# Heads 1 to 3: one weight sum by VectorE instead of an adding transfer, first splits of v two steps sooner, other spacing of the moves

## The chip, the cores and the metric

The kernel runs on one core of one Trainium2 chip. The metric is the device time of one execution in microseconds (us), the median of several runs. The core has a matrix engine (TensorE, PE in the profile), VectorE (DVE), ScalarE (ACT), GpSimd (POOL) and SyncE (SP); SP, ACT and POOL also issue transfers (DMAs), each through a queue of its own, onto the same 16 DMA engines.

## The reference

One decoder block over 512 tokens with a model width of 1024: a gated short convolution and an mLSTM branch with 4 heads read the same normalised input, are merged by sigmoid gates, and a gated embedding follows. Cut to what matters here:

```python
hn = rmsnorm(x, g_mix)
proj = einsum('bsd,de->bse', hn, w_in)
(xa, ba, ca, za, q, k, v, o, zb, ig, fg, ga, gb) = split(proj, ...)
ya = ba * causal_short_conv(ca * xa, conv_w, conv_b)
ya = einsum('bsc,cd->bsd', ya * silu(za), w_a_out)
hb = rmsnorm(mlstm_chunkwise(q, k, v, ig + b_i, fg + b_f), g_head)
yb = einsum('bsv,vd->bsd', sigmoid(o) * hb * silu(zb), w_b_out)
merged = sigmoid(ga) * ya + sigmoid(gb) * yb
x = x + einsum('bsd,de->bse', merged, w_o)
x = x + sigmoid(einsum(rmsnorm(x, g_ple), w_ple_gate)) * einsum(p, w_ple)
out = rmsnorm(x, g_final)
```

All of it is float32. Each head has 256 columns of q and k and 512 columns of v and o.

## The kernel before, in words

**Three matmuls for one.** A float32 operand is split into a high part, which TensorE takes exactly, and a low part, the rest. ScalarE writes the high part (`whi`, line 180) and VectorE subtracts it from the source (`wlo`, line 181); `mm3` (lines 231 to 235) multiplies high by high, high by low and low by high (L233, L234, L235 in the profile).

**Seven products for eight.** Most weight blocks come in pairs, and `pair` with `strassen` multiplies a 2 x 2 arrangement of blocks with seven products (a Strassen-Winograd scheme). The four weight chunks b11, b21, b12, b22 of a pair are 512 x 512 (1 MB each). For v and o of head h, b11 and b21 are the two halves in depth of v's weights, b12 and b22 those of o's. The seven right-hand operands are, in this order: operand 0, b11; operand 1, b21; operand 2, b11+b12; operand 3, b22; operand 4, that plus b22; operand 5, b12+b22; operand 6, operand 4 plus b21. So there are four sums, each made in place in a chunk's buffer (`wraw`, four buffers). A sum that `pair` marks None is an adding transfer: GpSimd issues a DMA (`add_chunk`, line 156) that reads the chunk from HBM once more and adds it to what lies in the buffer, in two halves of 512 KB. A sum that it marks `dve` is a VectorE addition of two buffers, in two halves too (line 185).

**The order of the work** is written out by hand. Product j has two halves, i = 0 and 1, for the two upper blocks of 128 tokens; after the matmuls of a half comes one *step* (`step` and `tick`), so that a pair has 14 steps, s1 to s14. In a step come, in this order: the tasks newly handed over (copies out of PSUM), one half of the split of the next operand (`split_half`: the high part on ACT, the low part on DVE, then the sums that hang on that operand), and one advance of every generator in `active`, the oldest first. Operand j+1 is therefore split in the two steps of product j, and the adds of an operand follow directly on its split. The sums hang on the operands so: b11+=b12 on operand 0; b12+=b22 on operand 1 where it is a transfer and on operand 3 where it is VectorE's; b11+=b22 on operand 2; b11+=b21 on operand 4. The loads of the next chunks are issued by SP (line 148) as soon as an operand's last use is past (`done`). Every engine runs its instructions in the order in which they were written.

**The stages.** `head(h)` runs four times. In heads 0 and 2 the pair v/o is followed by a pair for the gate zb of this and the next head and then by a pair for the merge gates (`sink_gate`); between heads 1 and 2 lies a pair for q and k. While the v/o pair runs, `scores` (started with it) makes the decay-weighted scores on ACT, DVE and, with 96 matmuls of up to 512 columns over the heads, PE; `scored` (line 990) then has GpSimd load the stored gate of an odd head (`gty` from `z_d`, line 994).

**sink_vo** (line 971) takes the results of the v/o pair. For v (n == 0) it waits for some steps (4 for the first two token blocks of heads 1 to 3), takes the buffer `vv`, splits the result into it (line 978 on ACT, line 981 on DVE) and leaves it for the weighted sums. For o it multiplies sigmoid(o) into the gate (lines 983 to 987). The copy of token block 0 is handed over in s3, its sum `c` is made in s4, its sink starts in s5; with 4 waiting steps the split stands in s9, that of block 1 in s10.

**finish(h)** (line 840) turns the finished head into the layout that the last projection wants: VectorE transposes 32 x 32 blocks (`turn`, line 812) into a buffer `yc`, 16 *moves* copy blocks within it (line 821 on ACT, line 819 on DVE; for head 3 into the buffer `m`), and `put` (line 824) stores the result in HBM (`yt_d`). `yc` and `vv` share one buffer (tag "vv"): the next head's `vv` can only be written when the stores of `yc` have read it. For heads 0 and 2 `finish` does half the tokens in 8 steps of moves, stores them (`put(0)`), transposes the other half and moves it in 6 steps that ACT and DVE share; its last store is issued by ACT in s3 of the next head's v/o pair. Head 1's two stores are issued by ACT in s3 of head 2's v/o pair. Head 3's moves run in the first pair of the convolution stage, from s9 on; that stage's `ya` (lines 408 and 410) shares the two tags "qk" and "vv". `recut` (heads 1 and 3) reads q and k back from HBM and splits them.

The list of moves is a list of pairs, one a step: (moves on ACT, moves on DVE).

Of the kernel before, what the change touches and what calls it, by code (L numbers as in the profile page):

```python
# [22 lines left out]
DV = 512  # L23
# [4 lines left out]
Q, K, V, O, ZB = 4096, 5120, 6144, 8192, 10240  # L28
# [8 lines left out]
def hybrid_block(ctx, tc, x, p, g_mix, w_in, conv_w, conv_b, w_a_out, b_gates, g_head,  # L37
# [24 lines left out]
    w_in_v = w_in[0].rearrange("(kt p) n -> p kt n", p=P)  # L62
# [9 lines left out]
    def chunk(view, k0, pieces):  # L72
        got, pos = [], 0
        for c, n in pieces:
            got.append((view[:, k0:k0 + HC, c:c + n], slice(0, HC), slice(pos, pos + n)))
            pos += n
        chunks.append(got)
        return len(chunks) - 1
# [5 lines left out]
    def pair(view, p1, p2, on_dve=0):  # L84

        where = ((p1, 0), (p1, HC), (p2, HC), (p2, 0)) if on_dve == 2 else ((p1, 0), (p1, HC), (p2, 0), (p2, HC))
        b11, b21, b12, b22 = (chunk(view, k, p) for p, k in where)
        if on_dve == 2:  # L90
            b12, b22 = b22, b12
        e2, e3 = (dve if on_dve >= n else None for n in (2, 1))
        t3 = [(b12, b22, e3)]
        operands.extend([(b11, [(b11, b12, None)]), (b21, [] if e3 else t3), (b11, [(b11, b22, e2)]),
                         (b22, t3 if e3 else []), (b11, [(b11, b21, e2)]), (b12, []), (b11, [])])
# [6 lines left out]
    qk_block(1)  # L102
    qk_block(0)
    for h in range(NH):
        pair(w_in_v, [(V + h * DV, DV)], [(O + h * DV, DV)])
        if h % 2 == 0:
            pair(w_in_v, [(ZB + h * DV, DV)], [(ZB + (h + 1) * DV, DV)])
            pair(w_in_v, [((GB, GA)[h // 2], CW)], [((GB, GA)[h // 2] + CW, CW)], 2)
        elif h == 1:
            pair(w_in_v, *([(Q + i * DK, DK), (K + i * DK, DK)] for i in (2, 3)), 1)  # L110
# [126 lines left out]
    def cut(hi, lo, src, scale=None):  # L237

        if scale is None:
            act.activation(hi, src, AF.Copy)  # L240
            dve.tensor_tensor(lo, src, hi.bitcast(F32), ALU.subtract)
        else:
            act.activation(hi, src, AF.Copy, scale=scale)
            dve.scalar_tensor_tensor(lo, src, scale, hi.bitcast(F32), ALU.mult, ALU.subtract)
# [38 lines left out]
    def temp(tag, name=None, dt=F32):  # L283

        return tp.tile([P, S], dt, name=name or tag, tag=tag, bufs={"c": 3}.get(tag, 2))
# [509 lines left out]
    def ptile(u, j, t):  # L795
        a = POFF[j] + (t - j) * P
        return u[:, a:a + P]
# [30 lines left out]
    def moves(move, plan):  # L828

        todo = deque(range((P // B) ** 2))  # L830
        for n_act, n_dve in plan:
            for i in range(max(n_act, n_dve)):
                if i < n_act:
                    move(todo.popleft(), False)
                if i < n_dve:
                    move(todo.popleft(), True)
            yield
        assert not todo

    def finish(h, y, tools):  # L840

        turn, move, put, _ = tools or turning(h, False, m[:, :2, :] if h == NH - 1 else None)
        if h % 2 == 0:
            yield from moves(move, [(2, 0), (2, 0), (3, 0), (3, 0), (2, 0), (1, 0), (2, 0), (1, 0)])
            put(0)
            for t in (2, 3):
                turn(y, t)
                yield
            yield from moves(move, [(1, 2), (1, 2), (0, 2), (0, 2), (1, 2), (1, 2)])
            put(1, nc.scalar)  # L850
            return
        for _ in range(4):
            yield
        for ts in ((0,), (1,), (2,), (3,)) if h == 1 else ((0, 1), (), (2,), (3,)):
            for t in ts:
                turn(y, t)
            yield
        yield from moves(move, [(1, 1)] * 8 if h == 1 else [(3, 0), (3, 1), (2, 1), (1, 1), (2, 2)])
        for i in range(2):
            put(i, nc.scalar if h == 1 else nc.gpsimd)  # L860

    def qk_tile():
        both = hp.tile([P, 2, 4, S], F32R, name="qk", tag="qk", align_bytes=256)
        return [both[:, i] for i in range(2)]
# [83 lines left out]
    def head(h, qk):  # L948
        vv = []

        def sink_qk(n, t, src):

            fs, ps = slice(2 * (t % 2), 2 * (t % 2) + 2), slice(t // 2 * H2, (t // 2 + 1) * H2)
            src = src.rearrange("p (f s) -> p f s", f=2)
            if n == 1:
                nc.gpsimd.dma_start(qk_d[h + 1][:, fs, ps], src)
                return
            for _ in range(4 if t < 2 else 0):
                yield
            if not qk:  # L960
                qk.extend(qk_tile())
            cut(*[u[:, fs, ps] for u in qk], src)
            yield

        if h == 2:
            strassen(hn_lhs, sink_qk, True)
        pr = [hq2.tile([P, 1280], F32R, name=f"pr{i}", align_bytes=256) for i in range(2)]
        pp = hq2.tile([P, 1280], F32, name="pp")
        gt = []

        def sink_vo(n, t, src):
            if n == 0:
                for _ in range(4 if t < 2 and h else 0):
                    yield
                if not vv:
                    both = hp.tile([P, 2, NT, DV], F32R, name="vv", tag="vv", align_bytes=256)
                    vv.extend(both[:, i] for i in range(2))
                act.activation(vv[0][:, t, :], src, AF.Copy)
                if t < 2:
                    yield  # L980
                dve.tensor_tensor(vv[1][:, t, :], src, vv[0][:, t, :].bitcast(F32), ALU.subtract)
            elif h % 2:
                so = temp("e", "so")
                act.activation(so, src, AF.Sigmoid)
                dve.tensor_tensor(gt[0][:, t, :], gt[0][:, t, :], so, ALU.mult)
            else:
                act.activation(gt[0][:, t, :], src, AF.Sigmoid)
            yield

        def scored():  # L990
            both = hp.tile([P, 2, NT, DV], F32, name="gty", tag="qk", align_bytes=256)
            gt.extend(both[:, i] for i in range(2))
            if h % 2:
                nc.gpsimd.dma_start(gt[0], z_d[h])

        active.append(scores(h, qk, pr, pp, scored))
        strassen(hn_lhs, sink_vo)
        gt, y = gt

        def weighted_sum(t, ps):  # L1000
            dve.tensor_scalar(y[:, t, :], ps, inv[:, t:t + 1], None, ALU.mult)
            junk = temp("e", "junk")
            act.activation(junk, y[:, t, :], AF.Square, accum_out=hss[:, t:t + 1])
            yield

        for t in range(NT):
            ps = ps_x.tile([P, S], F32, name="pv", tag="x")
            for j in range(t + 1):
                mm3(ps, [ptile(u, j, t) for u in pr], [u[:, j, :] for u in vv], j == 0, j == t)
            step(weighted_sum(t, ps))  # L1010

        def norm(t):
            dve.scalar_tensor_tensor(y[:, t, :], y[:, t, :], hr[:, t:t + 1], gt[:, t, :], ALU.mult, ALU.mult)

        def rsqrt():
            a, r, e = htmp
            dve.tensor_scalar(a, hss, 1.0 / DV, EPS, ALU.mult, ALU.add)
            pool.tensor_tensor(r, a, mhalf, ALU.pow)
            yield
            newton(e, a, r)  # L1020
            dve.tensor_tensor(hr, r, e, ALU.mult)
            for t in range(NT) if h % 2 else ():
                norm(t)
                if t == 1:
                    yield

        def sink_z(n, t, src):
            sz = temp("e", "sz")
            act.activation(sz, src, AF.Sigmoid)
            if n == 1:  # L1030
                dve.tensor_tensor(src, sz, src, ALU.mult)
                nc.gpsimd.dma_start(z_d[h + 1][:, t, :], src)
                yield
                return
            dve.tensor_tensor(sz, sz, src, ALU.mult)
            dve.tensor_tensor(gt[:, t, :], gt[:, t, :], sz, ALU.mult)
            yield
            norm(t)
            yield
            if t < 2:  # L1040
                yield
                if not tools:
                    tools.extend(turning(h, True))
                tools[0](y, t)
                yield

        tools = []
        active.append(rsqrt())
        if h % 2 == 0:
            strassen(hn_lhs, sink_z)  # L1050
        return y, tools
# [462 lines left out]
```

## Time and profile before

| | |
|---|---|
| median of 3 runs | 847.54 us (846.37 to 850.4) |
| profiled execution, whole | 846.08 us |
| its span, first to last instruction | 844.0 us |
| PE busy | 829.3 us (98%) |
| DVE busy | 673.2 us (80%) |
| ACT busy | 526.0 us (62%) |
| POOL busy | 219.6 us (26%) |
| DMA traffic | 173.87 MB |

Times in the profile are us from the first instruction. A row of the timeline is: start, duration, engine, line, operation, output <- inputs with their shapes, and in brackets the idle time of the engine before it with what ended it. A group's row is: line, engine, operation, shapes, count | busy us, mean ns of one | idle time before. A matmul's shown duration (0.39 us for 512 columns) overlaps that of the next: while nothing is waited for, such matmuls start every 0.23 us, so a delay of up to some 0.16 us between two of them doesn't show as idle time.

### The profile page before, as it was taken

Reading aid. Unit: us, or ns where it says so; the run is one execution under the profiler, and the core shown is the slowest. Engines: PE = TensorE matmul, PEld = TensorE weight load, DVE = VectorE, ACT = ScalarE, POOL = GpSimd, SP = SyncE. Lnnn points to the kernel's source line nnn. Section 1 sums busy time; section 2 is a strip of 40 time slices with the busy share of each in tenths; the row PEclk is TensorE's granted clock in tenths of the full one; section 3 lists DMA queues with packets and bytes.
Section 4 is the critical chain, followed back from the end, with each engine's and each line's share of the span. In section 5 each row is a group of like instructions: output and inputs, shape, how many; then the busy total and the mean of one; then the engine's idle time right before and its main releaser. Section 6 shows DMA issues by size and latency. Waiting matters only on the chain.

```text
span 844.0 us, 12126 instructions
## 1 busy us (share of the span) xinstructions
PE 829.3 (98%) x4520; PEld 720.5 (85%) x4520; DVE 673.2 (80%) x931; ACT 526.0 (62%) x779; POOL 219.6 (26%) x219
## 2 busy tenths in 40 slices
PE   9999999999999999999999999999999999999996
PEld 7888888888889978888877999999998888888885
DVE  5788767998688758789859899897985687999565
ACT  6467665778655766567766585555457356667553
POOL 5203122214125321320412234433411212121031
PEclk9999999999999999999999999999999999999999
DMA  9748789769979898995997789899889488999502
GB/s 312 266 148 183 155 217 222 196 211 249 253 156 190 223 253 187 252 218 159 253 235 201 136 196 228 188 184 182 182 260 374 102 194 221 279 255 233 185 1 99
DMA packets 104259, 173.87 MB, mean 206 GB/s; under 512 B 5697, under 2 KB 47221, under 8 KB 103433
## 3 DMA queue, kind: packets, MB, share of 16 engines
q0 software_dynamic: 40768, 72.43, 45.3%
q1 hardware_dynamic: 59792, 94.64, 33.9%
q10 hardware_dynamic: 3640, 6.04, 2.4%
q8 instruction: 35, 0.57, 0.3%
q14 instruction: 24, 0.19, 0.1%
HBM read 156.30 MB, written 16.79 MB: 205 GB/s over the span
## 4 chain that ended last, share of the span: by engine, by line
PE 72%; DMA 10%; issue 9%; DVE 4%; ACT 3%; POOL 2%; SPq 0%; POOLq 0%; DVEq 0%; ACTq 0%
PE mm L234 22%; PE mm L235 22%; PE mm L233 22%; DMA wraw<-in_w_in 8%; DVE wlo L181 2%; ACT whi L180 1%; PE pv L234 1%; PE pv L233 1%; PE pv L235 1%; DMA gty<-z_d 1%; DMA xin<-in_x 1%; POOL sg_d L782 1%; POOL wraw L156 0%; PE ptk L1307 0%; PE pth L1188 0%
## 5 line engine op out<-in xcount | busy, mean ns | idle before, releaser
L181 DVE TENSOR_TENSOR wlo<-wraw,whi 128x1024 fp32r<-128x1024 f32 x244 | 299.5, 1228 | 98.6 <-ACT whi L180 92.8
L180 ACT ACTIVATE whi<-wraw 128x1024 fp32r<-128x1024 f32 x246 | 257.8, 1054 | 96.6 <-PE mm L235 34.2
L156 POOL DMA_DIRECT2D wraw<-in_w_in x112 | 138.3, 1424 | 297.2 <-DVE wlo L181 204.4
L234 PE MATMUL mm<-wlo,hs 128*128 128x512 f32 x256 | 100.4, 392 | 1.7 <-DVE wlo L181 1.5
L233 PE MATMUL mm<-whi,hs 128*128 128x512 f32 x256 | 100.2, 391 | 1.1 <-ACT whi L180 0.9
L235 PE MATMUL mm<-whi,hs 128*128 128x512 f32 x256 | 99.8, 390 | 0.0
L346 ACT ACTIVATE s<-mm 128x512 f32<-128x512 f32 x84 | 50.1, 597 | 76.3 <-PE mm L235 75.1
L233 PE MATMUL mm<-hn_hi,whi 128*128 128x256 f32 (+1 forms) x304 | 93.5, 307 | 0.0
L235 PE MATMUL mm<-hn_hi,wlo 128*128 128x256 f32 (+1 forms) x304 | 93.3, 307 | 0.1
L234 PE MATMUL mm<-hn_lo,whi 128*128 128x256 f32 (+1 forms) x304 | 93.0, 306 | 0.0
L235 PE MATMUL mm<-hs,wlo 128*128 128x256 f32 x320 | 90.8, 284 | 0.0
L233 PE MATMUL mm<-hs,whi 128*128 128x256 f32 x320 | 90.8, 284 | 0.0
L234 PE MATMUL mm<-hs,whi 128*128 128x256 f32 x320 | 90.7, 284 | 0.0
L234 PE MATMUL mm<-wlo,hn_hi 128*128 128x512 f32 x192 | 75.0, 391 | 1.7 <-DVE wlo L181 1.7
L233 PE MATMUL mm<-whi,hn_hi 128*128 128x512 f32 x192 | 74.8, 390 | 0.0
L235 PE MATMUL mm<-whi,hn_lo 128*128 128x512 f32 x192 | 74.8, 390 | 0.0
L233 PEld LDWEIGHTS mm<-hs,whi 128*128 128x128 f32 x320 | 61.5, 192 | 0.0
L234 PEld LDWEIGHTS mm<-hs,whi 128*128 128x128 f32 x320 | 61.5, 192 | 0.0
L235 PEld LDWEIGHTS mm<-hs,wlo 128*128 128x128 f32 x320 | 61.5, 192 | 0.0
L235 PEld LDWEIGHTS mm<-hn_hi,wlo 128*128 128x128 f32 x304 | 58.1, 191 | 3.2 <-DVE wlo L181 0.3
L234 PEld LDWEIGHTS mm<-hn_lo,whi 128*128 128x128 f32 x304 | 58.2, 191 | 2.4
L233 PEld LDWEIGHTS mm<-hn_hi,whi 128*128 128x128 f32 x304 | 58.2, 191 | 2.3
(345 smaller groups left out, 1723.8 us busy)
## 6 DMA issues: line engine op xcount, KB each, us to landing
wraw<-in_w_in SPq DMA_DIRECT2D x32, 1024.0 KB, 5.6
wraw<-in_w_in POOLq DMA_DIRECT2D x52, 512.0 KB, 7.9
wraw<-in_w_in SPq DMA_DIRECT2D x48, 512.0 KB, 5.2
wraw<-in_w_in POOLq DMA_DIRECT2D x60, 256.0 KB, 5.7
wraw<-in_w_b_out SPq DMA_DIRECT2D x7, 1024.0 KB, 6.8
wraw<-in_w_b_out POOLq DMA_DIRECT2D x12, 512.0 KB, 6.6
wraw<-in_w_o SPq DMA_DIRECT2D x5, 1024.0 KB, 7.1
wraw<-in_w_a_out SPq DMA_DIRECT2D x4, 1024.0 KB, 5.0
```

The lines of the kernel that those rows point to most:

```text
L156: nc.gpsimd.dma_start(raws[to][:, ks, cs], src[:, ks, :], accum_op=ALU.add)
L180: act.activation(hi, t, AF.Copy)
L181: (e_lo or dve).tensor_tensor(lo, t, hi.bitcast(F32), ALU.subtract)
L233: pe.matmul(ps, lhsT=a[0], rhs=b[0], start=first, stop=False, **kw)
L234: pe.matmul(ps, lhsT=a[0], rhs=b[1], start=False, stop=False, **kw)
L235: pe.matmul(ps, lhsT=a[1], rhs=b[0], start=False, stop=last, **kw)
L346: act.activation(to[i], src, AF.Copy, scale=scale)
L782: nc.gpsimd.dma_start(sg_d[g + n][:, t, :], sg)
```

## The change

Three things are edited, in four places:

- For heads 1 to 3, `pair` is called with on_dve = 1 (head 0 keeps 0). With 1, the sum b12+=b22 is no longer two adding transfers behind operand 1, but two VectorE additions (line 185) behind the two halves of operand 3. The other three sums stay adding transfers. The order of loads stays.
- sink_vo waits 2 steps instead of 4 for the first two token blocks of v in heads 1 to 3.
- The 16 moves are spread otherwise: in the first phase of `finish` for heads 0 and 2, with the same number of steps, and for head 3 over 7 steps instead of 5, with 10 moves on ACT and 6 on DVE instead of 11 and 5.

```diff
     for h in range(NH):
-        pair(w_in_v, [(V + h * DV, DV)], [(O + h * DV, DV)])
+        pair(w_in_v, [(V + h * DV, DV)], [(O + h * DV, DV)], min(h, 1))
...
         if h % 2 == 0:
-            yield from moves(move, [(2, 0), (2, 0), (3, 0), (3, 0), (2, 0), (1, 0), (2, 0), (1, 0)])
+            yield from moves(move, [(2, 0), (2, 0), (1, 0), (1, 0), (2, 0), (2, 0), (3, 0), (3, 0)])
             put(0)
...
-        yield from moves(move, [(1, 1)] * 8 if h == 1 else [(3, 0), (3, 1), (2, 1), (1, 1), (2, 2)])
+        yield from moves(move, [(1, 1)] * 8 if h == 1 else [(2, 0), (2, 1), (1, 1), (1, 1), (1, 1), (2, 1), (1, 1)])
         for i in range(2):
             put(i, nc.scalar if h == 1 else nc.gpsimd)
...
             if n == 0:
-                for _ in range(4 if t < 2 and h else 0):
+                for _ in range(2 if t < 2 and h else 0):
                     yield
```

## The prediction

> **What bounds the kernel now.** I read the page first, then busy times by windows, then the chain of waits, and last the instructions at each gap.
>
> ```profile
> PE 829.3 (98%) x4520; PEld 720.5 (85%) x4520; DVE 673.2 (80%) x931; ACT 526.0 (62%) x779; POOL 219.6 (26%) x219
> ```
>
> PE is busy for 829.3 of 844.0 us, and the change leaves every matmul as it is. So it can only gain where PE waits, and it loses wherever it makes PE wait anew. The windows show where that is: six stretches of 18 us, the first and the fifth as references.
>
> ```profile
> core 0 of [0], span 844.0 us
> core 0: us, PE busy (x) PEld busy (x) DVE busy (x) ACT busy (x) POOL busy (x), PEclk, DMA share, GB/s
> 380.00:398.00 18.00, 18.00 (x81) 14.90 (x80) 16.77 (x17) 14.58 (x24) 1.62 (x3) 1.00 0.47 146
> 219.50:237.50 18.00, 17.40 (x76) 13.78 (x75) 15.96 (x34) 14.21 (x20) 2.99 (x3) 1.00 0.99 265
> 309.50:327.50 18.00, 17.07 (x75) 13.60 (x74) 15.14 (x33) 13.65 (x20) 2.39 (x2) 1.00 0.83 204
> 437.00:455.00 18.00, 15.27 (x64) 11.46 (x63) 15.40 (x26) 13.24 (x20) 2.98 (x3) 1.00 0.80 208
> 510.00:528.00 18.00, 18.00 (x153) 18.00 (x152) 16.62 (x25) 8.80 (x12) 6.76 (x7) 1.00 1.03 248
> 490.00:508.00 18.00, 17.87 (x149) 17.67 (x148) 16.12 (x25) 16.62 (x24) 5.09 (x6) 1.00 0.79 174
> ```
>
> Read the counts, not the busy times, since a matmul's shown duration covers part of a delay. An undisturbed stretch holds 81 matmuls of 512 columns, 18.00 / 81 = 0.222 us each. The v/o pair of head 1 (second row) holds 76, of head 2 75, of head 3 64: 5, 6 and 17 fewer, so 1.1, 1.3 and 3.8 us are lost there. In the convolution stage matmuls have 256 columns (153 in 18 us, 0.118 each); around 500 us, where head 3's moves run, 4 are missing, 0.5 us. That is 6.7 us in all, each row uncertain by about one matmul. The granted clock is 1.00 in every row, so nothing of this is clock.
>
> What PE waits for stands in the chain for head 3:
>
> ```profile
> 420.78 14.91 DMA wraw<-in_w_in
> ...
> 442.52 8.82 DMA gty<-z_d
> ```
> ```profile
> 441.55 0.51 PE L234 MATMUL mm<-wlo,hs 128*128 128x512 f32 x1 [0.76 <-DVE wlo L181]
> ...
> 453.92 0.50 PE L234 MATMUL mm<-wlo,hn_hi 128*128 128x512 f32 x1 [1.22 <-DVE wlo L181]
> ```
>
> The first wait is for operand 4: its sum (b11+=b22) is an adding transfer that takes 14.91 us to land, then come ACT's split and DVE's low part, and PE has run dry. The second (453.92) follows from it: GpSimd issues the gate's load `gty` behind the adds of operand 4, it lands at 442.52 + 8.82 = 451.34, and DVE, with the low part of operand 6 queued behind, stands at it.
>
> Why are the adds late? GpSimd's rows for head 3, first the two halves of b12+=b22, then of b11+=b22:
>
> ```profile
> L156 POOL DMA_DIRECT2D wraw<-in_w_in x2: 1792/2050/2307, 414.4 to 415.2; - x2
> ...
> DMA to landing us min/median/max: 14.4/15.8/17.1
> ```
> ```profile
> L156 POOL DMA_DIRECT2D wraw<-in_w_in x2: 1194/1194/1194, 420.8 to 425.2; - x2
> ...
> DMA to landing us min/median/max: 14.0/14.5/14.9
> ```
>
> They land at 414.4 + 14.4 = 428.8, 415.2 + 17.1 = 432.3, 420.8 + 14.9 = 435.7 and 425.2 + 14.0 = 439.2: one after the other, 3.4 to 3.5 us apart, like a queue. The two that are needed last (operand 5) stand ahead of the two that PE waits for.
>
> **The change, part by part.**
>
> *The transfers removed.* Six of 512 KB, two a head. If the adds go through in turn, those of b11+=b22 land two places sooner, 2 x 3.45 = 6.9 us; the second then at 432.3. That it could land no sooner after its issue than `gty` did, which had little beside it, gives the other bound: 425.2 + 8.8 = 434.0, 5.2 us sooner. Both exceed the 2.6 us (3.8 less the 1.22 at 453.92) that this wait costs in head 3, and the 1.1 and 1.3 us that heads 1 and 2 lose altogether. I take the queue, and this wait as gone in all three heads. The adds of operand 4 and `gty` behind them are issued as much sooner as operand 4's second low part is ready, 4.2 us by the next part, and what uses `gty` moves ahead by 2.6 us; that leaves 1.6 us, against the 1.22 us of idle time at 453.92 and its hidden part. So this wait goes as well.
>
> By the Trainium skill, page "DMA: Bandwidth & Descriptors", section "Anatomy of one DMA — SWDGE (gpsimd) path", a transfer takes about 2.0 us and its bytes at 436 GB/s, which would make 3.2 us of one half and 2.4 us of relief from two; the sum would then be just covered in head 3, with nothing to spare. Here the same transfers take 14 us to land and follow each other by 3.45 us, so the trace does not agree, and I go by it.
>
> *The additions added.* Two a head behind the low parts of operand 3, in VectorE's queue:
>
> ```profile
> L185 DVE TENSOR_TENSOR wraw<-wraw,wraw 128x1024 f32<-128x1024 f32 x24 | 29.3, 1222 | 2.7 <-DMA wraw<-in_w_b_out 2.4
> ...
> L821 ACT ACTIVATE yc<-yc 32x256 f32<-32x256 f32 x40 | 16.6, 414 | 0.7
> ...
> L821 ACT ACTIVATE m<-yc 32x512 f32<-32x512 f32 x11 | 6.9, 630 | 0.9 <-DVE yc L812 0.8
> ```
> ```profile
> 427.76 1.23 DVE L181 TENSOR_TENSOR wlo<-wraw,whi 128x1024 fp32r<-128x1024 f32 x1 [1.70 <-ACT whi L180]
> 428.90 0.68 DVE L925 SCALAR_TENSOR_TENSOR pp<-sc,e 128x512 f32<-128x512 f32 x1
> 430.06 1.23 DVE L181 TENSOR_TENSOR wlo<-wraw,whi 128x1024 fp32r<-128x1024 f32 x1 [0.48 <-ACT whi L180]
> 431.21 0.55 DVE L925 SCALAR_TENSOR_TENSOR pp<-sc,e 128x384 f32<-128x384 f32 x1
> 436.81 1.23 DVE L181 TENSOR_TENSOR wlo<-wraw,whi 128x1024 fp32r<-128x1024 f32 x1 [5.05 <-ACT whi L180]
> 437.95 0.69 DVE L922 TENSOR_TENSOR pr<-pp,pr 128x512 fp32r<-128x512 f32 x1
> 438.55 0.42 DVE L925 SCALAR_TENSOR_TENSOR pp<-sc,e 128x256 f32<-128x256 f32 x1
> ```
>
> Six times 1.222 = 7.3 us on DVE. In head 3 the two stand behind the low parts at 427.76 and 430.06, and DVE is idle for 5.05 us soon after. That cover shrinks when the wait goes, so I lay the new queue out: low part to 428.99, addition to 430.2, `pp` 430.9, low part 432.1, addition 433.3, `pp` 433.9, first low part of operand 4 to 435.1, `pr` and `pp` 436.2, second to 437.4. PE now gets that last one only for 441.55, and lost 2.6 us by waiting, so it would want it at about 439: 1.5 us to spare. Cost on PE nothing; if the cover were gone, each addition would cost 1.22 us. The next chunk's load on SP waits for the addition instead of the low part, 1.2 us later, with two products of time before its use. Operand 5's own sum is then ready by DVE's order, before ACT comes to it.
>
> *v two steps sooner.* The split of v stands in s7 and s8, beside operand 4's, instead of s9 and s10. The same instructions, but ACT's first one now waits earlier for `yt_d`'s store out of the shared buffer. Queued behind it on ACT is the second half of operand 4's split, and PE behind that. The critical head is 2, where head 1 is stored by two transfers issued from ACT:
>
> ```profile
> L824 ACTq DMA_DIRECT2D yt_d<-yc x2: 377/692/1006, 291.9 to 292.3; - x2
> ...
> DMA to landing us min/median/max: 13.7/17.0/20.3
> ```
> ```profile
> 311.80 1.06 ACT L180 ACTIVATE whi<-wraw 128x1024 fp32r<-128x1024 f32 x1 [2.81 <-DMA wraw<-in_w_in]
> ...
> 315.03 0.62 ACT L978 ACTIVATE vv<-c 128x512 fp32r<-128x512 f32 x1
> ```
>
> The later store lands at 292.3 + 20.3 = 312.6, before the split of v at 315.03 now. Two steps of 12 matmuls (5.3 us) sooner, and without the 1.3 us lost between, it is asked for at about 308.4. With two adds of this head gone, I expect the store 5.2 to 6.9 us sooner as well, at 305.7 to 307.4, since it shares the engines with them: no cost, 1.4 us at worst (rivals). In return the buffers `c` of the first two blocks are free sooner, and two DVE instructions leave the crowded steps s10 and s11, where `gty` is used.
>
> By the Trainium skill, page "DMA: Bandwidth & Descriptors", section "Queues, rings and completion order", each DMA engine takes a packet from each queue in turn, so a store of small packets crawls as long as the adds' queue is never empty. The 20.3 us agree with that, and it is the reason to expect the store to gain from the adds' absence.
>
> *The moves.* In heads 0 and 2 the same sixteen of 0.414 us, in the same eight steps; three more stand in the last two of them, so `put(0)` leaves about 1.2 us later, two steps ahead of the moves that wait for it. Nothing on PE. For head 3, ACT does one move of 0.630 us less and no step has more than two on ACT (three before); by the fourth step of the moves three fewer stand ahead of ACT's splits, 1.9 us, against 0.5 us that PE loses there now. I take the 0.5 us as gained.
>
> *Sum:* 1.1 + 1.3 + 3.8 + 0.5 = 6.7 us. I take 0.4 us off, two matmuls' worth of uncertainty in the counts, all on the side of less: 6.3 us. The profiled execution took 846.08 us with 844.0 of span, so 839.8 us; the median of the runs shown is 1.46 us above it, 847.54, which gives 841.2 us.
>
> **The rivals.**
>
> *One of the places stays.* If the 2.2 us of the later place remain (1.22 us idle plus the hidden part in head 3, about as much of head 1's 1.1 as lies behind `gty`), or VectorE's additions cost PE 0.4 us a head because a step then holds more than DVE can do, the gain is some 4.3 us: 843.2 us. For it: DVE is busy for 15.1 to 16.0 of 18 us in these windows already. Against: its idle 5.05 us lie where the additions go.
>
> *The adds were not waiting for one another.* If the adds land late because all queues share the engines (DMA share 0.80 to 0.99), the space is filled by the loads and stores beside, and b11+=b22 comes only one or two us sooner. Then head 1's and the convolution's loss go, 1.6 us: 845.9 us, no change. Against: the even spacing of the four landings.
>
> *The store of yc takes the adds' place* (slower). If the store still lands at 312.6, ACT stands at v's split from about 308; then 0.62 for it, 1.06 and 1.23 for operand 4's second half: low part ready at 315.6, against 314.2 if ACT splits at 311.80 as now (1.06 + 1.23 and a little). That is 1.4 us more than now in head 2, with nothing gained elsewhere: 847.54 + 1.4 = 848.9 us. It decides once the store lands after about 310: PE wants that low part 1.3 us sooner than now, at 312.8, and 0.62, 1.06 and 1.23 lie ahead of it. Against: it needs the adds' removal to relieve nothing.
>
> **How the numbers follow.** A measurement of this kernel can tell about 0.5% (4.2 us) from no change. Forecast 0.57; one place stays 0.23, on both sides of 4.2 us in about equal parts; adds not waiting for one another 0.14; the store 0.06, of which 0.03 beyond 0.5%, if heads 1 and 3 were hit as well. Faster: 0.57 + 0.11 = 0.68; slower 0.03; same 0.29. The low end is the lowest run shown, 846.37 us, less the whole 6.7 and a little more: 839.0. The high end, 845.2, takes in the second case and the better part of the third.
>
> **What would show it.** Right: the eight adding transfers of each v/o pair of heads 1 to 3 become six; those of b11+=b22 land within 6 to 10 us; the matmul count in the 18 us after operand 4's start is 79 to 81 in all three heads; six more VectorE additions of 1.22 us. Wrong: ACT idle before the split of v, ended by the store (the slower rival); adds of b11+=b22 still landing after 12 us or more (adds not waiting for one another); PE waiting for DVE at steps s5 to s8 with DVE never idle (additions not covered).

## The result and the profile after

The changed kernel took 838.79 us (median of 6 runs, 837.97 to 839.90) beside 847.14 us for the kernel before in the same rounds (median of 6, 844.66 to 850.40). The ratio is 0.990, with a 95% interval of 0.9878 to 0.9922: faster by 0.8 to 1.2%. The forecast had the direction and the mechanism; its 841.2 us is 2.4 us too high, and the result lies 0.2 us below the low end of its range.

The profiled execution of the changed kernel took 839.31 us with a span of 837.2 us. Against the profiled execution of before (846.08 us) that is 6.77 us less; the forecast's sum of what PE loses was 6.7 us. The first line of the page, and the chain that ended last by engine, first of the kernel after, then the same chain line of before:

```profile
PE 826.9 (99%) x4520; PEld 720.6 (86%) x4520; DVE 680.7 (81%) x938; ACT 526.0 (63%) x778; POOL 212.8 (25%) x213
...
PE 94%; DVE 2%; DMA 1%; issue 1%; ACT 1%; POOL 0%; POOLq 0%; ACTq 0%
```
```profile
PE 72%; DMA 10%; issue 9%; DVE 4%; ACT 3%; POOL 2%; SPq 0%; POOLq 0%; DVEq 0%; ACTq 0%
```

DVE holds seven instructions more (six additions and a move), POOL six fewer (the transfers). The chain shows what that bought: a tenth of the span went through a DMA before, and now 1%.

The windows of after are cut so that each begins and ends at the same matmul as a window of before did; PE runs the same 4520 matmuls in the same order in both kernels, so the first column after the bounds is the time for the same work. First head 1, 2 and 3's v/o pair, then the convolution around the moves, then the two references:

```profile
core 0: us, PE busy (x) PEld busy (x) DVE busy (x) ACT busy (x) POOL busy (x), PEclk, DMA share, GB/s
220.15:236.93 16.78, 16.78 (x76) 13.89 (x74) 14.53 (x31) 11.90 (x17) 1.79 (x2) 1.00 0.94 249
308.87:325.41 16.54, 16.54 (x74) 13.70 (x73) 14.46 (x31) 11.66 (x17) 1.19 (x1) 1.00 0.79 178
434.76:449.04 14.28, 14.28 (x64) 11.82 (x63) 12.25 (x24) 9.80 (x14) 1.18 (x2) 1.00 0.87 222
483.87:501.51 17.64, 17.64 (x149) 17.64 (x148) 15.90 (x24) 15.37 (x22) 5.27 (x5) 1.00 0.85 183
503.55:521.63 18.08, 18.08 (x152) 18.06 (x151) 17.34 (x27) 8.83 (x12) 7.98 (x8) 1.00 1.03 246
377.77:395.91 18.14, 18.14 (x82) 15.02 (x80) 16.67 (x16) 14.55 (x24) 1.63 (x3) 1.00 0.43 135
```

What took 18.0 us each before (to one matmul) now takes 16.78, 16.54 and 14.28 us in the three pairs, 1.2, 1.5 and 3.7 us less, with PE busy for the whole of each stretch; the convolution gained 0.4 us; the references did not move (18.08 and 18.14, the bounds being cut to a matmul).

The two adding transfers of b11+=b22 in head 3, which took 14.0 and 14.9 us to land, as the source line's answer has them for the changed kernel:

```profile
L156 POOL DMA_DIRECT2D wraw<-in_w_in x2: 1228/1232/1237, 418.5 to 421.9; - x2
...
DMA to landing us min/median/max: 7.8/8.2/8.7
```

They land at 418.5 + 8.7 = 427.2 and 421.9 + 7.8 = 429.7. The gate's load behind them, in heads 1 and 3:

```profile
L994 POOL DMA_DIRECT2D gty<-z_d x2: 1059/1060/1062, 221.1 to 434.9; - x2
...
DMA to landing us min/median/max: 8.0/8.1/8.1
```

It takes as long as before (8.1 to 8.8), but is issued at 434.9 instead of 442.5 and lands at 443.0. VectorE's timeline in head 3, from the additions (L185) to the use of the gate (L985):

```profile
424.51 1.23 DVE L181 TENSOR_TENSOR wlo<-wraw,whi 128x1024 fp32r<-128x1024 f32 x1 [1.71 <-ACT whi L180]
425.65 1.22 DVE L185 TENSOR_TENSOR wraw<-wraw,wraw 128x1024 f32<-128x1024 f32 x1
426.79 0.69 DVE L925 SCALAR_TENSOR_TENSOR pp<-sc,e 128x512 f32<-128x512 f32 x1
427.39 1.22 DVE L181 TENSOR_TENSOR wlo<-wraw,whi 128x1024 fp32r<-128x1024 f32 x1
428.52 1.22 DVE L185 TENSOR_TENSOR wraw<-wraw,wraw 128x1024 f32<-128x1024 f32 x1
429.66 0.55 DVE L925 SCALAR_TENSOR_TENSOR pp<-sc,e 128x384 f32<-128x384 f32 x1
430.30 1.22 DVE L181 TENSOR_TENSOR wlo<-wraw,whi 128x1024 fp32r<-128x1024 f32 x1
...
432.62 1.23 DVE L181 TENSOR_TENSOR wlo<-wraw,whi 128x1024 fp32r<-128x1024 f32 x1 [0.17 <-ACT whi L180]
...
444.60 0.70 DVE L985 TENSOR_TENSOR gty<-gty,so 128x512 f32<-128x512 f32 x1
```

This is the queue that the prediction laid out: low part, addition, `pp`, low part, addition, `pp`, then operand 4. VectorE has hardly any idle time left there, the 5.05 us before operand 4 are gone, and the last row has no bracket: the gate is used without a wait.

Head 1's stores out of the shared buffer, issued by ACT in head 2:

```profile
L824 ACTq DMA_DIRECT2D yt_d<-yc x2: 377/454/530, 291.2 to 291.6; - x2
...
  ACT vv L978: 0.7, 1
...
DMA to landing us min/median/max: 9.6/12.3/15.0
```

The later one lands 15.0 us after its issue, at 306.6, instead of 20.3 us. ACT still waits for it, for 0.7 us, and PE doesn't notice.

### The profile page after: what moved, and what is told of

It reads as the page before. It is cut to its first block, busy times and chain, and to the rows that moved or that the text cites. A ratio compares the mean times of both kernels' runs of the same rounds, so it can differ in the third digit from the quotient of the medians.

```text
span 837.2 us, 12110 instructions
## 1 busy us (share of the span) xinstructions
PE 826.9 (99%) x4520; PEld 720.6 (86%) x4520; DVE 680.7 (81%) x938; ACT 526.0 (63%) x778; POOL 212.8 (25%) x213
## 4 chain that ended last, share of the span: by engine, by line
PE 94%; DVE 2%; DMA 1%; issue 1%; ACT 1%; POOL 0%; POOLq 0%; ACTq 0%
PE mm L233 29%; PE mm L234 29%; PE mm L235 29%; DMA wraw<-in_w_in 1%; PE pv L235 1%; PE pv L233 1%; PE pv L234 1%; PE sc L235 1%; PE sc L234 1%; PE sc L233 1%; PE ptk L1307 0%; PE pth L1188 0%; PE pt L550 0%; PE mm L491 0%; DVE xin L545 0%
## 5 line engine op out<-in xcount | busy, mean ns | idle before, releaser
L156 POOL DMA_DIRECT2D wraw<-in_w_in x106 | 129.3, 1395 | 294.7 <-DVE wlo L181 200.1
```

The source lines that it names most:

```text
L156: nc.gpsimd.dma_start(raws[to][:, ks, cs], src[:, ks, :], accum_op=ALU.add)
```

## The experiments

The theory: PE waited for GpSimd's queue. The adds that are needed last stood ahead of those needed first, and the gate's load stood behind those; the change takes the first ones out. The rivals: it is the 3 MB less (the engines' load) and not the order; the earlier split of v or the other spacing of the moves brings part of the gain; VectorE's additions cost something that hides in the total.

Since the matmuls come in the same order in every kernel, the loss of a pair is the time between the same two matmuls in its PE timeline, less the shortest time seen for it (21.82 us for a stretch of head 1's pair, 22.50 in head 2, 58.12 in head 3). The table is worked out in this way from one profiled execution of each kernel (not from a single view); the last column takes the three losses from that execution's time.

```
kernel          profiled us   lost in head 1, 2, 3   sum    the rest
before             846.08      1.19  1.49  3.90      6.58    839.50
before_b           846.37      2.85  0.29  3.52      6.66    839.71
before_c           845.59      1.45  1.19  3.24      5.88    839.71
before_d           848.04      2.49  2.42  3.65      8.56    839.48
after              839.31      0.00  0.00  0.00      0.00    839.31
sums_only          838.49      0.00  0.00  0.02      0.02    838.47
more_sums          841.30      0.00  0.00  1.69      1.69    839.61
no_sums            848.42      1.81  5.24  2.88      9.93    838.49
v_only             848.49      2.32  3.43  3.40      9.15    839.34
late_transfer      842.68      1.55  0.00  2.28      3.83    838.85
gty_only           844.79      2.89  1.15  1.35      5.39    839.40
late_gty           841.90      1.29  0.00  1.60      2.89    839.01
extra_add          843.12      1.58  0.00  2.65      4.23    838.89
```

The rest is 838.5 to 839.7 us in all thirteen, however the times differ. So what these kernels differ by lies in the three v/o pairs, to about a microsecond.

**sums_only: the kernel before with the pair's edit alone.**

```diff
-        pair(w_in_v, [(V + h * DV, DV)], [(O + h * DV, DV)])
+        pair(w_in_v, [(V + h * DV, DV)], [(O + h * DV, DV)], min(h, 1))
```

> Only the sum b12+b22 of heads 1 to 3 goes to VectorE; v's splits stay in s9 and s10, the moves stay as before. Queue theory (the two transfers stand ahead of those that PE waits for): the waits in the three v/o pairs go as they did with the whole change, 6.2 us (1.1, 1.3, 3.8); only the 0.5 us around 500 us stay. About 6 us faster than before, and the adds of b11+=b22 land within 8 to 10 us. Rival (the earlier split of v is what frees the crowded steps s10 and s11): the first waits go, those on gty's step stay, 2.2 us; 4 us faster.

838.74 us (6 runs, 838.49 to 839.95), ratio 0.9905 (0.9885 to 0.9924). That is the whole change's result: the sum by VectorE is the change. The same stretch of the convolution that took 26.07 us before and 25.68 us after takes 25.95 us here, so the moves bring 0.27 us on top of it, which the time can't tell.

**no_sums and v_only: the other edits without the sum.** no_sums is the changed kernel without the pair's edit; v_only is the kernel before with only the earlier split of v.

```diff
-                for _ in range(4 if t < 2 and h else 0):
+                for _ in range(2 if t < 2 and h else 0):
```

> The whole change without the sum: v's splits in s7 and s8, the new moves, all four sums by transfers. Queue theory: the store of yc and the adds land as before (312.6 and 311.8 us on head 2), so ACT stands at v's split and head 2 loses up to 1.4 us more; the convolution stage gains 0.5 us; heads 1 and 3 as before or up to 1 us better by the less crowded steps. In all within 1.5 us of before. Rival (the earlier split is a gain by itself): 2 to 4 us faster.

> The kernel before with only v's first splits two steps sooner. Theory (ACT stands at the store of yc in head 2 and TensorE's clock falls after the gap): all of the loss of the run without the sum comes from here, 1.5 to 4 us slower than before, with some 5 us lost in head 2's pair. Rival (the new moves make that loss): no slower than before.

no_sums: 848.68 us (12 runs), ratio 1.0031 (1.0011 to 1.0050). v_only: 848.63 us (12 runs), 1.0031 (1.0017 to 1.0045). Both are slower, by the same 2.6 us, so it is v's step and not the moves that costs it. For no_sums that is more than the 1.5 us expected. For v_only it is within what was expected, but head 2 loses 3.43 us there and not some 5, and the granted clock does not fall in its profile (last section). This is the prediction's slower rival, on its own: ACT's first split of v in head 2 waits for the store (no_sums, then v_only):

```profile
313.99 0.63 ACT L978 ACTIVATE vv<-c 128x512 fp32r<-128x512 f32 x1 [4.54 <-DMA yt_d<-yc]
314.52 1.04 ACT L180 ACTIVATE whi<-wraw 128x1024 fp32r<-128x1024 f32 x1
```
```profile
313.72 0.63 ACT L978 ACTIVATE vv<-c 128x512 fp32r<-128x512 f32 x1 [3.50 <-DMA yt_d<-yc]
```

The row below it is operand 4's second half, queued behind, as that rival said. In the changed kernel the wait is the 0.7 us shown above: the sum's edit frees the store, so the two edits belong together, and the earlier v then costs nothing and brings nothing that can be measured.

**late_transfer: the same sum at the change's place, but still by transfers.** The two adds of b12+=b22 are issued behind operand 3 instead of operand 1 in heads 1 to 3 (all else as in the changed kernel). Bytes and transfers are those of before.

```diff
+        late = on_dve == -1
...
-        ... (b21, [] if e3 else t3), (b11, [(b11, b22, e2)]), (b22, t3 if e3 else []), ...
+        ... (b21, [] if e3 or late else t3), (b11, [(b11, b22, e2)]), (b22, t3 if e3 or late else []), ...
...
-        pair(w_in_v, [(V + h * DV, DV)], [(O + h * DV, DV)], min(h, 1))
+        pair(w_in_v, [(V + h * DV, DV)], [(O + h * DV, DV)], -min(h, 1))
```

> The whole change, but the sum b12+b22 stays an adding transfer; it is only issued behind operand 3's splits, where the change has VectorE's additions, and so behind the transfers of b11+=b22. The same bytes and the same number of transfers as before. Queue theory (order within GpSimd's queue decides): b11+=b22 lands as early as with the change, 5 to 6 us of the 6.8 are kept, a little is lost if operand 5 or gty now wait for the two late ones. Rival (all queues share the DMA engines and the total load decides): no more than 1.5 us faster than before.

842.37 us (10 runs, 840.45 to 845.02), ratio 0.9949 (0.9932 to 0.9966): about half of the gain, with not a byte less. That lies between the two expectations, 5 to 6 us and 1.5 at the most. In head 3 the transfers of b11+=b22 land 9.0 and 8.2 us after their issue, as with the change, and PE does not wait at operand 4 in any of the three heads. Head 2 loses nothing, heads 1 and 3 lose 1.55 and 2.28 us. But for 0.5 us in head 3, which stand ahead of all this (a low part at 412.6), they are lost at the gate's load, now behind the two late adds (its row and landing, then VectorE's wait):

```profile
L995 POOL DMA_DIRECT2D gty<-z_d x2: 1059/1060/1062, 219.9 to 436.1; - x2
...
DMA to landing us min/median/max: 12.0/12.1/12.2
```
```profile
448.40 0.69 DVE L986 TENSOR_TENSOR gty<-gty,so 128x512 f32<-128x512 f32 x1 [2.48 <-DMA gty<-z_d]
```

12.1 us to land instead of 8.1. The order alone removes the wait for operand 4; the transfers that are left then delay the gate instead.

**gty_only and late_gty: the gate's load by SP instead of GpSimd**, in the kernel before and in late_transfer.

```diff
-                nc.gpsimd.dma_start(gt[0], z_d[h])
+                nc.sync.dma_start(gt[0], z_d[h])
```

> The kernel before with only gty's load moved from GpSimd's queue to SP's. Queue theory: the second place in heads 1 and 3 goes (0.7 and 1.5 us in the profile of before), the waits for operand 4 stay: 1 to 2.5 us faster. Rival (gty is late because the engines are full): no difference beyond 0.2%.

> late_transfer once more, with the gate's load gty issued by SP instead of GpSimd, so that it doesn't stand behind the adding transfers. Still the bytes and the transfers of before, nothing added to VectorE. Queue theory (what remained in late_transfer, 1.5 us in head 1 and 2.2 in head 3, is gty behind two more adds): those 3 us go as well; 6 to 7.5 us faster than before, as fast as the change within 1.5 us. Rival (the DMA engines' load): as late_transfer, 4 us faster than before.

gty_only: 843.92 us (12 runs), ratio 0.9978 (0.9962 to 0.9995), 1.9 us faster, as expected. In its profile the load lands after 8.2 us and VectorE uses the gate without a wait in both heads. Head 3 loses 1.35 us instead of 3.90. Head 1 still loses 2.89: 0.9 us at operand 4 and 1.9 us at the later place, where ACT waits 2.12 us for an adding transfer and PE then for a copy queued behind it on ACT. The expectation, that the later place goes in both heads, holds for head 3 alone.

late_gty: 840.79 us (6 runs), 0.9934 (0.9912 to 0.9956), by the medians 1.6 us better than late_transfer and 2 us short of the change; the intervals of late_gty and late_transfer overlap. I had expected it within 1.5 us of the change. Why it is short:

```profile
L995 SPq DMA_DIRECT2D gty<-z_d x2: 339/339/339, 218.2 to 433.6; - x2
...
DMA to landing us min/median/max: 13.9/13.9/13.9
```
```profile
447.62 0.69 DVE L986 TENSOR_TENSOR gty<-gty,so 128x512 f32<-128x512 f32 x1 [1.02 <-DMA gty<-z_d]
```

SP's queue holds two loads of the next chunk ahead of it, and the gate's load lands after 13.9 us, no better than behind the adds. So this kernel doesn't remove the wait for the gate. What is left, 1.29 and 1.60 us, stands at the low part behind that wait in both heads. The place in SP's queue alone does not explain it: in gty_only the same two loads stand ahead and the gate's load takes 8.2 us. What differs is that the two loads ahead take 14.2 us to land in head 3 of late_gty and 9.8 us in gty_only. The late adds are the likely cause, though on another queue; no run separates them from the rest. So order explains the half of the gain that late_transfer keeps. For the other half the rival stands: it needs the late transfers gone, and whether by their place in GpSimd's queue or by the load that they put on the DMA engines stays open, since no kernel here has the late transfers and a gate's load with nothing ahead of it.

**extra_add: the changed kernel with one more VectorE operation** of the same shape behind each of the six additions (the maximum of b22 with itself, in place, which leaves b22 as it is).

```diff
+                if c in twice:
+                    eng.tensor_tensor(raws[c][:, ks, :], raws[c][:, ks, :], raws[c][:, ks, :], ALU.max)
```

> The whole change with one more VectorE instruction of the same size behind each of the six additions (the maximum of b22's buffer with itself, which changes nothing), so 7.3 us more on VectorE, at the same places. By the step count of the prediction 1.5 us are to spare in head 3 and 2.4 more are put in: it costs 0 to 1 us a head against the change, 0 to 3 us in all, so still 4 to 8 us faster than before. Rival (VectorE's additions have no cover, each costs its 1.2 us): 7 us slower than the change, no faster than before.

841.96 us (6 runs, 841.08 to 843.12), ratio 0.9938 (0.9917 to 0.9959), 3.2 us above the change for 7.3 us more work on VectorE, a little more than the 0 to 3 us expected; in the profile head 2 loses nothing, heads 1 and 3 lose 1.58 and 2.65 us instead of up to 1. So the additions of the change are covered and there is little cover left. The loss doesn't come by the way that I had in mind, operand 4's low part (PE waits 0.2 us there). That part being later, so are the adds behind it on GpSimd, and the gate behind those:

```profile
448.92 0.69 DVE L989 TENSOR_TENSOR gty<-gty,so 128x512 f32<-128x512 f32 x1 [1.74 <-DMA gty<-z_d]
```

The load leaves at 439.6 instead of 434.9, takes 9.3 us instead of 8.1, lands at 448.9 instead of 443.0, and the low part of operand 6 stands behind the wait.

**more_sums: the same sum by VectorE in head 0's v/o pair and both zb pairs as well.**

```diff
-        pair(w_in_v, [(V + h * DV, DV)], [(O + h * DV, DV)], min(h, 1))
+        pair(w_in_v, [(V + h * DV, DV)], [(O + h * DV, DV)], 1)
...
-            pair(w_in_v, [(ZB + h * DV, DV)], [(ZB + (h + 1) * DV, DV)])
+            pair(w_in_v, [(ZB + h * DV, DV)], [(ZB + (h + 1) * DV, DV)], 1)
```

> The change with the sum b12+b22 by VectorE in head 0's v/o pair and in both gate pairs (zb) too: six more additions, six adding transfers fewer. Theory (PE only gains where it waited for those transfers; the changed kernel waits nowhere in these pairs, only up to 1.2 us behind them at 168 to 171 us): the same as the change within 0.2%, 0 to 1 us better. Rival (each adding transfer less is a gain, since the load of the DMA engines limits): 3 us better and more.

838.61 us (6 runs, 838.01 to 841.30), ratio 0.9908 (0.9884 to 0.9933): the same as the change. Six transfers of 512 KB less again, and nothing gained, since PE doesn't wait there. It speaks against the rival that every transfer less is a gain. The profiled execution is the slowest of the six, and it loses 1.69 us in head 3, in a pair that this run leaves as the change has it: 1.0 us of it behind the gate, for which VectorE waits 1.78 us. So the gate's wait can come back in single executions of the changed pair.

**before_b, before_c, before_d: three more profiled executions of the kernel before,** unchanged, to see what its scatter is made of.

> The kernel before once more, unchanged, for a second profile. Theory (the profiled execution of before was a mild one; in others the same waits are longer, or long enough that the granted clock falls after them): where its time is above 847 us, the matmul counts in the v/o pairs of heads 1 to 3 are lower than 76, 75 and 64, and a lower clock stands behind a gap of 2 us or more. Rival (the spread of before lies elsewhere, in the start, the convolution or the end): the three counts are the same within 2 and the difference lies outside the three pairs.

> The kernel before, unchanged, for a third profile; as for the second one: the losses in the three v/o pairs follow its time by about 1 us for 1 us (theory), or stay at 6 to 7 us whatever its time (rival).

> The kernel before, unchanged, for a fourth profile; the same two expectations.

846.37, 845.59 and 848.04 us. The table has them: the losses in the pairs differ from execution to execution (head 1 by 1.7 us, head 2 by 2.1 us), in sum from 5.9 to 8.6 us, and the time goes with the sum: the rest agrees to about 0.2 us. In these four executions the time scatters because these waits scatter. The fall of the clock that was expected behind longer gaps is not seen: the granted clock is 1.00 through the three pairs in all four. In others it may well add to the time. Of 55 other runs of the kernel before, the 12 with a mean granted clock of 0.994 or 0.995 have a median of 848.05 us, and the 43 with 0.996 to 0.998 one of 845.77; no trace shows one of the 12.

## Why the prediction was right and where it was wrong

*What PE loses, and where:* right. 1.1, 1.3, 3.8 and 0.5 us were forecast; the same matmuls show 1.19, 1.49, 3.90 and 0.39 us, 6.97 in all. The wait for operand 4 went in all three heads, as taken, and so did the one at the gate, though its margin is small: it is back in the profiles of more_sums and extra_add.

*The transfers removed:* right. 5.2 to 6.9 us sooner was forecast; they land 6.2 us sooner after their issue (14.9 to 8.7, 14.0 to 7.8). The gate's load was to leave 4.2 us sooner within head 3; it leaves 7.6 us sooner, of which heads 1 and 2 give 2.7, so 4.9. That the order does it for operand 4, with not a byte less, is what late_transfer shows. At the gate the queue is not shown to be the whole reason (late_gty).

*The additions:* right, at no cost on PE in the profiled execution. The 1.5 us to spare at operand 4 were rather too few: with 2.4 us more a head PE loses 0.3 us there in head 3 and nothing in heads 1 and 2. But the margin that counts lies elsewhere: it is the gate's load that runs out first, and at it stand some 1.5 us in each of heads 1 and 3 in extra_add.

*v two steps sooner:* the store was to land at 305.7 to 307.4 and landed at 306.6; no cost, right. The rival's price was wrong: 1.4 us more in head 2 than before, where v_only loses 1.9 more (3.43 less 1.49) and no_sums 3.75, and the clock has a part in that (last section).

*The moves:* the 0.5 us taken as gained were 0.4 in the profile. With the sum alone 0.27 us of it stay lost, so that much is the moves' doing.

*The sum* was 6.3 and came to 6.77 between the two profiled executions. The 0.4 us "all on the side of less" were taken off on the wrong side, since the counts had read the losses too small, by 0.27 us in all.

*The step that failed:* "the median of the runs shown is 1.46 us above it, 847.54, which gives 841.2 us". The offset of before's median to its profile was carried over to the changed kernel. Of 61 runs of the kernel before the median is 846.45 us (842.16 to 850.45); three runs had put it 1.1 us too high. And what scatters there, as far as the four profiles of before show it, are the waits that the change removes: in the same rounds the six runs of the changed kernel keep within 1.9 us (837.97 to 839.90) and the six of before within 5.7, and the changed kernel's median lies 0.5 us *below* its profiled execution. The profiled 839.8 us forecast was 0.5 us from the 839.31 measured; the 841.2 made of it was not. The low end fell with it, "the lowest run shown, 846.37 us, less the whole 6.7 and a little more": the lowest run is one with smaller waits, so the whole of another execution's waits can't be taken off it, and it was the lowest of three. To take the profile's waits off the profile's own time, 846.08 less 6.7, and to leave it there, would have given 839.4.

What is left of the difference between 7.7 us (the medians 846.45 and 838.79) and 6.77 us (the profiles) is 0.37 us by which before's profile lies below its median and 0.52 us by which after's lies above. For the latter one place can be named: a stretch of head 0's gate pair that takes 66.67 us in sums_only and late_transfer, 67.13 in before and 67.86 in this execution of after. Some of head 0's moves stand there, but their spacing doesn't decide it: the seven executions with the old spacing take 66.67 to 67.53 us, the six with the new one 66.67 to 67.86. What does was not settled.

## What to carry to other kernels

An in-order queue that issues adding transfers should issue them in the order in which their results are needed; one that is needed late and issued early delays all behind it, and half of this gain was to be had by order alone. What the late transfers then delay is a second question, and moving the delayed load to another queue did not settle it here. When a change removes waits, forecast the new time as the profiled execution's own time less the waits seen in that execution; don't add an offset that the same waits make, and expect the scatter to go as well. An edit that starts an engine's work sooner on a shared buffer should be tried with and without the edit that frees the buffer: here it costs 2.6 us without it and nothing with it.

## What the runs showed of the hardware

**The clock after a short gap.** In no_sums PE waits twice in head 2, and then runs at half rate:

```profile
312.88 0.39 PE L235 MATMUL mm<-whi,hs 128*128 128x512 f32 x1
315.62 0.50 PE L233 MATMUL mm<-whi,hs 128*128 128x512 f32 x1 [2.35 <-ACT whi L180]
316.88 0.80 PE L234 MATMUL mm<-wlo,hs 128*128 128x512 f32 x1 [0.76 <-DVE wlo L181]
317.47 0.63 PE L235 MATMUL mm<-whi,hs 128*128 128x512 f32 x1
317.89 0.63 PE L233 MATMUL mm<-whi,hs 128*128 128x512 f32 x1
...
319.60 0.63 PE L234 MATMUL mm<-wlo,hs 128*128 128x512 f32 x1
320.03 0.47 PE L235 MATMUL mm<-whi,hs 128*128 128x512 f32 x1
```
```profile
313.00:321.00 8.00, 4.89 (x14) 3.53 (x13) 5.41 (x10) 5.20 (x8) 1.19 (x1) 0.79 0.58 94
```

The second fence is the window around it: the granted clock is 0.79 on average where every window above has 1.00. It is 0.50 from 316.8 to 320.2 us, for 3.4 us. From 317.47 to 320.03 six matmuls start 0.427 us apart instead of 0.23. v_only has the same two waits, a little shorter, and keeps its clock:

```profile
315.35 0.50 PE L233 MATMUL mm<-whi,hs 128*128 128x512 f32 x1 [1.67 <-ACT whi L180]
316.61 0.50 PE L234 MATMUL mm<-wlo,hs 128*128 128x512 f32 x1 [0.76 <-DVE wlo L181]
316.94 0.40 PE L235 MATMUL mm<-whi,hs 128*128 128x512 f32 x1
317.17 0.39 PE L233 MATMUL mm<-whi,hs 128*128 128x512 f32 x1
```
```profile
313.00:321.00 8.00, 5.57 (x23) 4.08 (x23) 5.67 (x10) 5.43 (x9) 1.19 (x1) 1.00 0.71 111
```

With 0.68 us more of waiting, the next seven intervals were 1.5 us longer in all (from 316.88 to 320.03 in 3.15 us, where seven take 7 x 0.23 = 1.6). The Trainium skill, page "TensorE: Matmul & The Clock Gate", section "Part 1: The HAM clock gate (the "warmup" mystery)", gives 426.7 ns from start to start for matmuls of 512 columns while the array is cold, that is at half clock, and a window of about 3.4 us over which its activity is watched; the spacing of 0.427 us and the 3.4 us at half clock agree. By its section "HAM oscillation — how this bites in real kernels" the rule is to have no idle gaps of PE over about 3.4 us; here 2.35 and 0.76 us with one matmul between them were enough in one execution. Whether the length or the moment of the gap decided isn't shown by these two executions.

**The same transfer lands much later when others stand ahead of it or beside it.** The gate's load, always of the same size, took 8.1 us to land from GpSimd behind operand 4's adds and 12.1 us behind two more adds. From SP, behind the same two loads of a chunk, it took 8.2 us in gty_only and 13.9 us in late_gty, where the two late adds were under way on GpSimd's queue. The same adding transfers of b11+=b22 landed in 14.0 to 14.9 us behind two others, and in 7.8 to 8.7 us without them.
